# A feed-forward in two token groups, and the same in three passes whose first projection is seven products of half the features

## The chip, the cores and the metric

The kernel runs on one core of a Trainium2 chip. The time is device microseconds of one execution; the figure given is the median of three runs. A core has five engines with a queue of instructions each: TensorE (PE in the profile, its weight loads as PEld), VectorE (DVE), ScalarE (ACT), GpSimd (POOL) and SyncE (SP), which issues most transfers. An instruction that must wait for another engine waits on a semaphore at the head of its engine's queue.

## The reference

One decoder layer on 2048 prompt tokens and 32 sample tokens (8 sequences of 4): 1024 features, feed-forward width 2816.

```python
def swiglu(h, w_ffn_in, w_ffn_out):
    g, u = jnp.split(h @ w_ffn_in, 2, axis=-1)
    return (jax.nn.silu(g) * u) @ w_ffn_out

def trunk_layer(x, c, lw, mixer):
    sh1, sc1, g1, sh2, sc2, g2 = adaln_mods(c, lw['w_ada'], lw['b_ada'])
    h = rms_norm(x, lw['norm1_g']) * (1 + sc1) + sh1
    m, states = mixer(h)
    x = x + g1 * m
    h2 = rms_norm(x, lw['norm2_g']) * (1 + sc2) + sh2
    x = x + g2 * swiglu(h2, lw['w_ffn_in'], lw['w_ffn_out'])
    return x, states
```

The mixer (convolution branch, windowed attention, gates, an output projection) stands before the feed-forward; a final norm follows it. All inputs and outputs are float32.

## The kernel before

**Arithmetic.** Features lie on the 128 partitions, tokens along the free axis. Each projection's operand, weight or activation, is split in a high part (rounded to the matmul's 32-bit format, written by ScalarE) and a low part (the rest), and a product is three matmuls: high·high, high·low, low·high, accumulated in one PSUM bank. There are four such banks (`mm`).

**Groups.** The tokens go in two groups, one after the other: group 0 has 1024 tokens in two chunks of 512 columns, group 1 has 1056 in three of 352, the last 32 of which are sample tokens with their own modulation. A group runs `mixer_in`, `mixer_out` (which ends with the output projection "wo" and the residual x2), then `ffn`.

**Feed-forward.** For each of 22 tiles f of 128 hidden features ("G1"), the gate ("fg") and the up projection ("fu") each make 8 contraction tiles × 3 matmuls per chunk. ScalarE takes the gate's bank through Silu (L1434), VectorE multiplies the up bank with it (L90 is the helper that records VectorE and TensorE instructions), ScalarE and GpSimd split the product (L1442, L1443). After two tiles comes the second projection of the pair before ("G2", weights "fo"): for each chunk and each of 8 output tiles, 6 matmuls, and VectorE adds the result to x2 (`residual`). The order is G1 0, G1 1, then G1 2p, G2 p−1, G1 2p+1.

**Weights.** A plan lists the weight units in order of use, 1024 columns each. `w_dma` loads one raw unit by SyncE (512 KB, two raw buffers `wr`), `w_conv` splits it: ScalarE writes `wh` (L190), GpSimd subtracts for `wl` (L192). Four split units are held (`NBUF`). `w_prefetch` emits loads and splits as far as these buffers allow; it is called whenever a unit is taken and when one is given back (`w_done`). So a split's place in its engine's queue is fixed by where in the program the buffer is given back.

**Other work.** Generators in `bg` and `tasks` (norms, operand preparation, output) are stepped by `pump` after each accumulator tile, as far as a running estimate of VectorE's time is behind TensorE's. `norm2` forms the feed-forward's operands h2 (`scaled`, `modulate`, L678) during the end of `mixer_out`.

## Time and profile before

| | |
|---|---|
| median of three runs | 2958.16 us (2956.43 to 2958.36) |
| profiled execution | 2956.81 us, its span 2954.9 us, granted TensorE clock 0.981 |
| TensorE busy | 2826.6 us, 96% of the span |
| GpSimd busy | 1116.4 us, 38%, of which 658.7 in 256 weight splits (L192) |
| VectorE busy | 1432.5 us, 48% |
| ScalarE busy | 893.6 us, 30%, of which 264.5 in weight splits (L190) |

In a row of a group stand line, engine, operation, the tile written and those read, shapes, count, then the busy time and the mean nanoseconds of one, then the idle time of the engine just before and what ended it. In a row of a timeline stand start and duration in us. A row of a stretch has its length, then for each engine the busy time and the count, then the granted clock, the share of the transfer engines and GB/s. In a list of waits stand the total, the number and the longest.

## The change

**Three passes.** The feed-forward runs in three passes of two pieces of tokens: 2 × 336, 2 × 352, 2 × 352 (`PASSES`; `ffn(p)`). Pass 0 belongs to the end of group 0, passes 1 and 2 to that of group 1; piece (0,2) of group 0 is kept for pass 1. The pieces of x2 that must wait are written to DRAM (`x2_d`) and read again. All feed-forward weights are loaded once per pass, three times instead of twice. `mixer_out` works in the same pieces (`out`), so group 0's has three instead of two.

**Seven products.** In a pass the first projection is a 2×2 block product: (two pieces) × (two halves of 1024 features), with the gate and up tile as the two columns of weights. Strassen's scheme makes it of seven products of 4 contraction tiles × 3 matmuls instead of eight, on sums of operands and of weights. The sums of activations are formed once per pass (`f_values`, `f_build`, `f_split`: 16 values, 16 differences, 28 splits), the sums of weights for each tile f (`w_part`: s1, B and s2 ahead of product p6, one more, named P3 here, ahead of p3), and the results are combined per tile on VectorE from the banks (`f_gate`: one copy of p1 by ScalarE, seven sums, two products). The order is p1, p6, p7, p5, p2, p3, p4.

**Half units.** Each product's weight is half a unit of 512 columns; two halves share one split buffer, in order of use (`w_pair`), which is given back when both are done. Seven halves per f come of the two raw buffers of gate (a, raw0) and up (b, raw1), four more per pair from "fo". An extra raw buffer may be used once the operands are built (`raw_extra`). The second projection gives back its four halves at its end. The last two second projections stand at the end of a pass.
